# Gated linear attention: the two heads' products of a chunk regrouped by the number of rows they use

## The chip, the cores and the metric

The kernel runs on one core of one Trainium2 chip. The metric is device microseconds of one execution; the time before is the median of three runs. Beside them stands one profiled execution, from which every duration below is taken.

## The reference, cut to what matters

The kernel computes a whole decoder layer: a token mixer with three branches, a cross-attention and a mixture of experts. The change lies in the third branch of the mixer, gated linear attention, with 4 heads, 64 key columns and 128 value columns a head, 1024 tokens:

```
q_t = q * jnp.exp(cum)
k_t = k * jnp.exp(-cum)
attn = jnp.where(causal, jnp.einsum('bhnid,bhnjd->bhnij', q_t, k_t), 0.0)
intra = jnp.einsum('bhnij,bhnje->bhnie', attn, v)
k_dec = k * jnp.exp(cum[..., -1:, :] - cum)

def step(state, xs):
    qt_c, kd_c, v_c, cd_c = xs
    out = jnp.einsum('bhcd,bhde->bhce', qt_c, state)
    state = state * cd_c[..., None] + jnp.einsum('bhcd,bhce->bhde', kd_c, v_c)
    return state, out
```

The output of a chunk is its inner part (masked scores times values) plus what the state from the chunks before gives (queries times state).

## The kernel before, in words

gla_mix is called twice, once for each pair of heads. The keys and queries of a pair lie on 128 partitions, head 0 on rows 0 to 63 and head 1 on rows 64 to 127 (the list rows in the code), 1024 tokens along the free axis, in NT = 8 chunks of 128 tokens. All of its products are float32; each call is recorded as two weight loads and two matmuls.

The score part (L917 to L927) runs over head a, then over g, half of the chunks. Into one PSUM buffer of 128x4x128 it makes four products that use the 64 rows of the head (L923, 64 rows by 128 columns), then four that use 64 rows by 64 columns (L926); VectorE then copies the buffer under the mask into the scores AT of that head (L927). So the four groups a, g come one after the other, and each group holds two kinds of products.

Between, ScalarE and VectorE scale the queries and keys (L930 to L932), and TensorE transposes the keys (L938).

The chunk loop (L942 to L960) makes, for each chunk and head, po = qe times S (L947, 64 rows of the head, not for the first chunk) and adds AT times v to it (L948, all 128 rows); ScalarE copies po out (L949). Then for all but the last chunk the two heads' new key-value products go into one buffer, each on its own 64 columns (L954, 128 rows by 64 columns), and VectorE makes the next state S of it (L959, L957 for the first).

Around that, k.stream.fill(n) puts n steps of six matmuls each of the next projections into the program (L142 to L144, 128 rows by 128 columns, 512 moving columns): eight steps before the scores, two before the transposes, one in each chunk. A scheduler orders each engine's instructions when the kernel is built: the instruction that stands first in the program among those it takes to be ready. So the order on TensorE in the trace is not quite that of the program: L947 waits for S, and half of a step of projections stands ahead of it.

The pool k.ps has four PSUM buffers under the tag "s" that the scores, po and the state product share. Every buffer has the size of the largest tile of the tag, 128x4x128 float32.

After the second pair the kernel goes on with the projections up to the first head of the gated DeltaNet (gdn_mix), and so on to the end of the layer.

Of the kernel before, what the change touches and what calls it, by code (L numbers as in the profile page):

```python
# [8 lines left out]
F32 = mybir.dt.float32  # L9
# [35 lines left out]
def slot(k, name, shape=(128, T), dt=F32):  # L45

    return k.b4.tile(list(shape), dt, tag="b4", name=name)
# [611 lines left out]
def finish_out(k, on, sz, wc, oT, sq, spill=None):  # L659

    nc = k.nc
    ss = k.sm.tile([128, NT], F32, tag="rms_ss", bufs=2)
    for g in range(2):
        h = slice(g * 4, g * 4 + 4)
        nc.scalar.activation(sq[:, h], on[:, h], AF.Square)
        nc.vector.reduce_sum(ss[:, h], sq[:, h], axis=AX.X)
    r = k.sm.tile([128, NT], F32, tag="rms_r", bufs=2)
    rsqrt_cols(k, r, ss, NT, 128.0e-6)
    nc.vector.tensor_tensor(on, on, r[:, :, None].to_broadcast([128, NT, 128]), op=OP.mult)
    k.stream.fill(4)  # L670
    for g in range(2):
        ps = k.ptp.tile([128, 512], F32, tag="tp")
        for j in range(4):
            nc.tensor.transpose(ps[:, j * 128:(j + 1) * 128], on[:, g * 4 + j], k.ident)
        s = slice(g * HALF, (g + 1) * HALF)
        nc.vector.scalar_tensor_tensor(oT[:, s], ps, k.pcol[:, wc:wc + 1], sz[:, s], op0=OP.mult, op1=OP.mult)
    if spill is not None:
        nc.sync.dma_start(spill, oT)
# [210 lines left out]
def gla_mix(k, u, p, oT):  # L889
    nc = k.nc  # L890
    rows = (slice(0, 64), slice(64, 128))
    L = k.L

    def c3(t):
        return t.rearrange("p (c t) -> p c t", c=NT)

    def c4(t):
        return t.rearrange("p (c h t) -> p c h t", c=NT, h=2)

    c1, E, kt = c4(L.c1), c4(L.E), c3(L.kt)  # L900
    nc.vector.tensor_tensor_scan(L.c1, k.rm64, k.la[p], 0.0, OP.mult, OP.add)
    nc.scalar.activation(E, c1, AF.Exp, scale=1.0 / 16.0)
    nc.vector.scalar_tensor_tensor(u.q, L.E, 0.125, u.q, op0=OP.mult, op1=OP.mult)
    qt = c3(u.q)
    ee = k.sm.tile([128, NT, 2], F32, tag="l_ee", bufs=2)
    nc.vector.tensor_copy(ee, E[:, :, :, 63])
    cd = k.sm.tile([128, NT], F32, tag="l_cd", bufs=2)
    nc.vector.tensor_tensor(cd, ee[:, :, 0], ee[:, :, 1], op=OP.mult)
    nc.scalar.activation(E, c1, AF.Exp, scale=-1.0 / 16.0)
    nc.vector.tensor_tensor(L.kt, L.E, u.k, op=OP.mult)  # L910
    nc.vector.tensor_tensor(E, c1[:, :, :, 63:64].to_broadcast([128, NT, 2, 64]), c1, op=OP.subtract)
    nc.scalar.activation(E, E, AF.Exp, scale=1.0 / 16.0)
    nc.vector.tensor_tensor(u.k, L.E, u.k, op=OP.mult)
    kd = c3(u.k)
    k.stream.fill(8)

    for a in range(2):  # L917
        r = rows[a]
        for g in range(2):
            ps = k.ps.tile([128, 4, 128], F32, tag="s")  # L920
            for j in range(4):
                c = g * 4 + j
                nc.tensor.matmul(ps[:, j], kt[r, c], qt[r, c], start=True, stop=True)  # L923
            for j in range(4):
                c = g * 4 + j
                nc.tensor.matmul(ps[0:64, j, 64:128], kd[r, c, 0:64], qt[r, c, 64:128], start=True, stop=True)  # L926
            nc.vector.copy_predicated(L.AT[a][:, g * 4:g * 4 + 4], k.trii[:, None, :].to_broadcast([128, 4, 128]), ps)  # L927

    qe = c3(L.kt)
    nc.scalar.copy(qe[:, :, 0:64], qt[:, :, 0:64])  # L930
    nc.vector.tensor_tensor(qe[:, :, 64:128], qt[:, :, 64:128], ee[:, :, 0:1].to_broadcast([128, NT, 64]), op=OP.mult)
    nc.vector.tensor_tensor(kd[:, :, 0:64], kd[:, :, 0:64], ee[:, :, 1:2].to_broadcast([128, NT, 64]), op=OP.mult)  # L932
    kn = c3(L.E)
    k.stream.fill(2)
    for g in range(2):
        ps = k.ptp.tile([128, 4, 128], F32, tag="tp")
        for j in range(4):
            nc.tensor.transpose(ps[:, j], kd[:, g * 4 + j], k.ident)  # L938
        nc.scalar.copy(kn[:, g * 4:g * 4 + 4], ps)
    on = [c3(L.q2), c3(L.c1)]  # L940
    S = None
    for c in range(NT):  # L942
        for a in range(2):
            r = rows[a]
            po = k.ps.tile([128, 128], F32, tag="s")
            if S is not None:
                nc.tensor.matmul(po, qe[r, c], S[r], start=True, stop=False)  # L947
            nc.tensor.matmul(po, L.AT[a][:, c], u.v[a][:, c], start=(S is None), stop=True)  # L948
            nc.scalar.copy(on[a][:, c], po)  # L949
        k.stream.fill(1)  # L950
        if c < NT - 1:
            ps = k.ps.tile([128, 128], F32, tag="s")
            for a in range(2):
                nc.tensor.matmul(ps[rows[a]], kn[:, c, rows[a]], u.v[a][:, c], start=True, stop=True)  # L954
            Sn = L.small[:, 1 + c % 2]
            if S is None:
                nc.vector.tensor_copy(Sn, ps)  # L957
            else:
                nc.vector.scalar_tensor_tensor(Sn, S, cd[:, c:c + 1], ps, op0=OP.mult, op1=OP.add)  # L959
            S = Sn  # L960
    for a in range(2):
        finish_out(k, on[a], u.sz[a], 75, slot(k, "oc"), c3(L.kt), oT[2 * p + a])
# [1105 lines left out]
def hybrid_block(ctx, tc, ins, out):  # L2068
# [33 lines left out]
    with ExitStack() as c:  # L2102
        k.ps = c.enter_context(tc.tile_pool(name="psl", bufs=4, space=PSUM))
        for p in range(2):
            S.upto(f"l{p}")
            gla_mix(k, U[f"l{p}"], p, oT["c"])
# [114 lines left out]
```

## Time and profile before

| what | us |
|---|---|
| median of three runs | 2030.04 |
| lowest and highest of them | 2027.97, 2032.48 |
| the profiled execution | 2029.34 |
| its span, first to last instruction | 2027.6 |
| TensorE busy in the span | 1874.6 |

A row of the timeline gives the start, the time from the start of its first to the end of its last instruction, the engine, the line and operation, the tiles (out<-in), rows*columns of the array, the moving operand and the count; in brackets the idle time of the engine just before and what ended it. PE is the matmul, PEld the weight load of TensorE. Matmuls overlap in such rows: from the start of one to the start of the next is what one takes of the engine's time, and its own duration is longer.

### The profile page before, as it was taken

To read this page: it belongs to the slowest core of one execution; us is meant where nothing else is said; L and a number is where in the kernel's file an instruction comes from. 1 tells how busy PE (TensorE), PEld (TensorE's weight loads), DVE (VectorE), ACT (ScalarE), POOL (GpSimd) and SP (SyncE) were. 2 spreads that over 40 slices of the span, in tenths; PEclk is the share of its full clock that TensorE was granted. 3 is DMA by queue.
4 is the path that set the end of the run, shared out by engine and by line. 5 is a ranking of instruction groups with operands and counts; after the bars stand their busy time and mean duration, and the time that the engine had idled before them with its cause. 6 is when DMAs were issued, how large, how long until landed. Compare 5 with 4: busy or idle time off the path is not lost. (4 is left out here: it accounts for less than half of the span.)

```text
span 2027.6 us, 26514 instructions
## 1 busy us (share of the span) xinstructions
PE 1874.6 (92%) x9820; PEld 1521.3 (75%) x9820; DVE 1213.4 (60%) x2629; ACT 840.3 (41%) x1454; POOL 224.1 (11%) x261
## 2 busy tenths in 40 slices
PE   7999999999999999999989999899989689998890
PEld 6777787787877788888877788888877557876670
DVE  3244376676766543424455767544577648997885
ACT  3433232333332353535443312433421148876773
POOL 2000000000000010000003100000001222332310
PEclk8999999999999999999999999999999899999995
DMA  4113123232314122122525323710345577999995
GB/s 129 33 32 84 42 83 79 63 99 63 99 53 105 57 63 73 53 84 68 167 84 200 119 101 108 197 28 25 115 166 179 188 254 248 294 308 313 303 302 187
DMA packets 201653, 265.95 MB, mean 131 GB/s; under 512 B 24490, under 2 KB 132200, under 8 KB 201520
## 3 DMA queue, kind: packets, MB, share of 16 engines
q1 hardware_dynamic: 148992, 149.45, 23.6%
q10 hardware_dynamic: 39264, 86.07, 12.3%
q0 software_dynamic: 13264, 28.71, 6.0%
q8 instruction: 78, 1.28, 0.3%
q14 instruction: 55, 0.45, 0.1%
HBM read 228.95 MB, written 51.97 MB: 139 GB/s over the span
## 5 line engine op out<-in xcount | busy, mean ns | idle before, releaser
L142 PE MATMUL ps<-thh,hi 128*128 128x512 f32 x1152 | 467.7, 406 | 5.2 <-ACT hi L52 1.9
L143 PE MATMUL ps<-thl,hi 128*128 128x512 f32 x1152 | 456.4, 396 | 0.0
L144 PE MATMUL ps<-thh,lo 128*128 128x512 f32 x1152 | 455.7, 396 | 0.0
L142 PEld LDWEIGHTS ps<-thh,hi 128*128 128x128 f32 x1152 | 218.0, 189 | 51.5 <-issue 6.0
L144 PEld LDWEIGHTS ps<-thh,lo 128*128 128x128 f32 x1152 | 217.5, 189 | 45.8 <-issue 1.1
L143 PEld LDWEIGHTS ps<-thl,hi 128*128 128x128 f32 x1152 | 218.2, 189 | 38.8 <-issue 0.3
L1890 DVE TENSOR_TENSOR sl<-m_raw,sh 128x1024 fp32r<-128x1024 f32 x180 | 214.2, 1219 | 41.2 <-ACT sh L1887 31.6
L1887 ACT ACTIVATE sh<-m_raw 128x1024 fp32r<-128x1024 f32 x180 | 186.1, 1059 | 36.4 <-DMA acc<-m_y,r_big 13.0
L53 DVE TENSOR_TENSOR lo<-raw,hi 128x1024 fp32r<-128x1024 f32 x64 | 78.3, 1224 | 117.1 <-ACT hi L52 105.9
L52 ACT ACTIVATE hi<-raw 128x1024 fp32r<-128x1024 f32 x64 | 67.8, 1059 | 139.8 <-PE ps L143 120.1
L1646 PE MATMUL ps<-sl,m_xhi 128*128 128x512 f32 x240 | 97.6, 407 | 15.2 <-DVE sl L1890 14.5
L1645 PE MATMUL ps<-sh,m_xhi 128*128 128x512 f32 x240 | 101.1, 421 | 2.7 <-ACT sh L1887 2.7
L1647 PE MATMUL ps<-sh,m_xlo 128*128 128x512 f32 x240 | 95.9, 400 | 1.5 <-DVE m_xlo L1909 1.5
L783 DVE CUSTOM_DVE_ANT_0 f_P<-S,f_c 128x1024 f32<-128x1024 f32 (+7 forms) x64 | 48.4, 757 | 80.9 <-PE S L780 78.5
L1706 POOL DMA_INDIRECT acc<-m_y,r_big x32 | 60.3, 1883 | 205.8 <-ACT sh L1887 51.0
L1053 PE MATMUL ps<-ohi,hi 128*128 128x512 f32 x192 | 77.1, 402 | 1.5 <-DVE mt L1061 1.5
L791 ACT ACTIVATE f_P<-f_P,nm 128x1024 f32<-128x1024 f32 (+7 forms) x64 | 49.8, 778 | 65.7 <-DVE nm L783 65.4
L1055 PE MATMUL ps<-ohi,lo 128*128 128x512 f32 x192 | 75.5, 393 | 0.0
L1054 PE MATMUL ps<-olo,hi 128*128 128x512 f32 x192 | 75.3, 392 | 0.0
L1646 PEld LDWEIGHTS ps<-sl,m_xhi 128*128 128x128 f32 x240 | 45.9, 191 | 30.9 <-DVE sl L1890 22.4
L718 POOL TENSOR_SCALAR_AFFINE_SELECT f_c<-f_c 128x128 f32<-128x128 f32 x64 | 22.5, 351 | 388.8 <-DVE nm L783 363.6
L801 ACT COPY f_PT<-ps 128x512 f32<-128x512 f32 (+3 forms) x96 | 43.4, 479 | 46.1 <-PE ps L800 37.3
(489 smaller groups left out, 3733.2 us busy)
## 6 DMA issues: line engine op xcount, KB each, us to landing
raw<-in_w_in SPq DMA_DIRECT2D x64, 512.0 KB, 4.2
m_raw<-in_moe_w_down ACTq DMA_DIRECT2D x56, 512.0 KB, 5.9
m_raw<-in_moe_w_gate ACTq DMA_DIRECT2D x108, 256.0 KB, 5.9
m_raw<-in_moe_w_up ACTq DMA_DIRECT2D x108, 256.0 KB, 6.3
gate<-gt SPq DMA_DIRECT2D x24, 512.0 KB, 3.0
mt<-gate SPq DMA_DIRECT2D x24, 512.0 KB, 5.3
wraw<-in_xa_wkv SPq DMA_DIRECT2D x16, 512.0 KB, 7.5
m_raw<-in_moe_w_gate SPq DMA_DIRECT2D x20, 256.0 KB, 4.8
```

The source lines that it names most:

```text
L53: k.nc.vector.tensor_tensor(lo, src, hi.bitcast(F32), op=OP.subtract)
L142: k.nc.tensor.matmul(ps[:, :n], hi[:, d], xh, start=(d == 0), stop=False)
L143: k.nc.tensor.matmul(ps[:, :n], hi[:, d], xl, start=False, stop=False)
L144: k.nc.tensor.matmul(ps[:, :n], lo[:, d], xh, start=False, stop=(d == ND - 1))
L1053: nc.tensor.matmul(ps, whi[:, f], hi[:, s], start=(f == 0), stop=False)
L1054: nc.tensor.matmul(ps, whi[:, f], lo[:, s], start=False, stop=False)
L1055: nc.tensor.matmul(ps, wlo[:, f], hi[:, s], start=False, stop=(f == 3))
L1645: nc.tensor.matmul(ps, x[0], w[0], start=start, stop=False)
L1646: nc.tensor.matmul(ps, x[0], w[1], start=False, stop=False)
L1647: nc.tensor.matmul(ps, x[1], w[0], start=False, stop=stop)
L1887: nc.scalar.activation(w[e, i][0], raw[e][i], AF.Copy)
L1890: nc.vector.tensor_tensor(w[e, i][1], raw[e][i], w[e, i][0].bitcast(F32), op=OP.subtract)
```

## The change

The loops over heads move inward. In the scores g becomes the outer loop; both heads have a buffer, the eight products of L923 of a half come first, the heads alternating from product to product, then the eight of L926 in the same way, then both copies. In the chunk loop both po buffers are taken first; both heads' 128-row products (L948) come first and open the sum, then both heads' 64-row products (L947) close it, then both copies. No product, copy or load is added or removed.

```
-    for a in range(2):
-        r = rows[a]
-        for g in range(2):
-            ps = k.ps.tile([128, 4, 128], F32, tag="s")
-            for j in range(4):
-                c = g * 4 + j
-                nc.tensor.matmul(ps[:, j], kt[r, c], qt[r, c], start=True, stop=True)
-            for j in range(4):
-                c = g * 4 + j
-                nc.tensor.matmul(ps[0:64, j, 64:128], kd[r, c, 0:64], qt[r, c, 64:128], start=True, stop=True)
-            nc.vector.copy_predicated(L.AT[a][:, g * 4:g * 4 + 4], k.trii[:, None, :].to_broadcast([128, 4, 128]), ps)
+    for g in range(2):
+        ps = [k.ps.tile([128, 4, 128], F32, tag="s", name="ps") for a in range(2)]
+        for c in range(g * 4, g * 4 + 4):
+            for a, r in enumerate(rows):
+                nc.tensor.matmul(ps[a][:, c % 4], kt[r, c], qt[r, c], start=True, stop=True)
+        for c in range(g * 4, g * 4 + 4):
+            for a, r in enumerate(rows):
+                nc.tensor.matmul(ps[a][0:64, c % 4, 64:128], kd[r, c, 0:64], qt[r, c, 64:128], start=True, stop=True)
+        for a in range(2):
+            nc.vector.copy_predicated(L.AT[a][:, g * 4:g * 4 + 4], k.trii[:, None, :].to_broadcast([128, 4, 128]), ps[a])
...
     for c in range(NT):
+        po = [k.ps.tile([128, 128], F32, tag="s", name="po") for a in range(2)]
         for a in range(2):
-            r = rows[a]
-            po = k.ps.tile([128, 128], F32, tag="s")
-            if S is not None:
-                nc.tensor.matmul(po, qe[r, c], S[r], start=True, stop=False)
-            nc.tensor.matmul(po, L.AT[a][:, c], u.v[a][:, c], start=(S is None), stop=True)
-            nc.scalar.copy(on[a][:, c], po)
+            nc.tensor.matmul(po[a], L.AT[a][:, c], u.v[a][:, c], start=True, stop=S is None)
+        if S is not None:
+            for a, r in enumerate(rows):
+                nc.tensor.matmul(po[a], qe[r, c], S[r], start=False, stop=True)
+        for a in range(2):
+            nc.scalar.copy(on[a][:, c], po[a])
```

## Rows read from the trace of the kernel before

**Rows 1.** The page: the span, and part 1, busy time of each engine.

```profile
span 2027.6 us, 26514 instructions
PE 1874.6 (92%) x9820; PEld 1521.3 (75%) x9820; DVE 1213.4 (60%) x2629; ACT 840.3 (41%) x1454; POOL 224.1 (11%) x261
```

**Rows 2.** Busy time by stretch: length, then engines in order, PEclk, DMA.

```profile
120.00:265.00 145.00, 145.00 (x766) 110.37 (x766) 58.35 (x116) 42.48 (x84) 4.41 (x11) 1.00 0.20 51
```

**Rows 3.** Timeline of PE: the scores of the first pair, then of the second.

```profile
124.91 1.16 PE L923 MATMUL ps<-l_u,l_kt 64*128 64x128 f32 x8
126.00 0.68 PE L926 MATMUL ps<-l_u 64*64 64x64 f32 x8
...
131.67 0.50 PE L142 MATMUL ps<-thh,hi 128*128 128x512 f32 x1
...
218.16 1.16 PE L923 MATMUL ps<-l_u,l_kt 64*128 64x128 f32 x8
...
224.92 0.50 PE L142 MATMUL ps<-thh,hi 128*128 128x512 f32 x1
```

**Rows 4.** Timeline of PE at two instants: score products in flight.

```profile
125.12 0.50 PE L923 MATMUL ps<-l_u,l_kt 64*128 64x128 f32 x3
...
126.10 0.39 PE L926 MATMUL ps<-l_u 64*64 64x64 f32 x4
```

**Rows 5.** Timeline of PE over one chunk of the first pair.

```profile
138.60 0.49 PE L947 MATMUL po<-l_small,l_kt 64*128 64x128 f32 x2
139.01 0.49 PE L948 MATMUL po<-l_u,l_AT 128*128 128x128 f32 x2
139.43 0.48 PE L947 MATMUL po<-l_small,l_kt 64*128 64x128 f32 x2
139.85 0.49 PE L948 MATMUL po<-l_u,l_AT 128*128 128x128 f32 x2
...
140.63 0.40 PE L144 MATMUL ps<-thh,lo 128*128 128x512 f32 x1
140.96 0.44 PE L954 MATMUL ps<-l_u,l_E 128*64 128x128 f32 x4
141.33 0.50 PE L142 MATMUL ps<-thh,hi 128*128 128x512 f32 x1
141.66 0.39 PE L143 MATMUL ps<-thl,hi 128*128 128x512 f32 x1
...
142.22 0.48 PE L947 MATMUL po<-l_small,l_kt 64*128 64x128 f32 x2
```

**Rows 6.** Timeline of PE in a later stage: products on alternating 64-column halves.

```profile
714.97 0.55 PE L807 MATMUL ps<-f_PT,f_v 128*64 128x128 f32 x6
```

**Rows 7.** Lines L947 and L926: count, shortest, median and longest ns, first and last start.

```profile
L947 PE MATMUL po<-l_small,l_kt x56: 272/322/373, 138.6 to 255.3; 64*128 64x128 f32 x56
...
L926 PE MATMUL ps<-l_u x64: 218/218/267, 126.0 to 224.8; 64*64 64x64 f32 x64
```

**Rows 8.** Timeline of DVE and PE: the state, and the keys ahead of the transposes.

```profile
141.45 0.35 DVE L959 SCALAR_TENSOR_TENSOR l_small<-l_small,cd,ps 128x128 f32<-128x128 f32 x1 [3.33 <-PE ps L954]
...
131.78 0.73 DVE L927 COPY_PREDICATED l_AT<-l_small,ps 128x512 f32<-128x512 int32 x1
132.41 0.67 DVE L932 TENSOR_TENSOR l_u<-l_u,ee 128x512 f32<-128x512 f32 x1
...
134.32 0.39 PE L144 MATMUL ps<-thh,lo 128*128 128x512 f32 x1
134.55 0.27 PE L938 MATMUL ps<-ident,l_u 128*128 128x128 f32 x1
```

**Rows 9.** Timeline of ACT: copies of po out of PSUM.

```profile
139.54 0.27 ACT L949 COPY l_q<-po 128x128 f32<-128x128 f32 x1 [1.51 <-PE po L948]
```

**Rows 10.** Timeline after the branch: DVE, then PE, waits of the next stage.

```profile
310.42 0.69 DVE L517 TENSOR_REDUCE ss<-g_X 128x4 f32<-128x512 f32 x1 [4.98 <-ACT g_X L516]
...
348.84 0.36 PE L600 MATMUL ps<-g_Tn,g_LT 128*64 128x64 f32 x3 [1.87 <-DVE g_Tn L593]
```

## The prediction

> **What bounds the kernel now.** I read the page first: TensorE is busy for 1874.6 of 2027.6 us [rows 1]. That is an average over the whole layer, so the second view is the busy time of the stretch in which the changed branch runs: from 120 to 265 us matmuls cover all of the 145.00 us, the granted clock is 1.00 (the 2.4 GHz level), VectorE is busy for 58.35 and ScalarE for 42.48 us [rows 2]. So in this stretch only TensorE's own time counts. "Busy" doesn't say that it is busy at its best, though: matmuls overlap, and the third view, the timeline of TensorE, shows where one follows the other late. There the reader should compare distances from start to start.
>
> Products that use the same part of the array follow each other closely. Three of L923 span 0.50 us, and a matmul of this shape lasts 0.27, so they stand (0.50 - 0.27) / 2 = 0.11 us apart; four of L926 span 0.39, one lasts 0.22, so (0.39 - 0.22) / 3 = 0.06 apart [rows 4, 7]. Where the shape changes, the distance grows. In a chunk L947 starts at 138.60, L948 at 139.01, L947 at 139.43, L948 at 139.85 [rows 5]: 0.41 to 0.42 us for two matmuls that would take 0.22 at the close distance. Each visit to another shape thus costs 0.19 us: the second matmul comes 0.49 - 0.27 = 0.22 after the first, which is 0.10 late, and the next shape starts 0.20 after the second, which is 0.09 late. The same is seen where projections meet another shape: one of them and what follows it in the same shape start 0.23 apart (134.32 to 134.55) [rows 8], but 0.33 ahead of L954 (140.63 to 140.96) and 0.33 behind it (141.33 to 141.66) [rows 5]. Six shape changes lie in one chunk of 142.22 - 138.60 = 3.62 us.
>
> One more thing is in these rows: the four matmuls of L954, two heads on two 64-column halves, take 0.44 us, and the next line starts 0.37 after their first [rows 5]. Six of L807, also alternating between column halves, take 0.55 us; one by one at 0.11 they would take 5 x 0.11 + 0.27 = 0.82 [rows 6]. The two halves run at the same time: three pairs, two distances.
>
> **The change part by part.** Nothing is added or removed, so the whole effect is order.
>
> The chunk loop. New order in a chunk: L954 of the chunk before, both L948 (four matmuls, same shape as the projections), projections, both L947, projections. Four shape changes are left of six. Summing a chunk from the rows of before:
> - L954 with its way out: 140.96 to 141.33, 0.37.
> - Four matmuls of L948, the first of them after a change: 0.22 + 3 x 0.11 = 0.55.
> - Six projections at 0.23: 1.36.
> - Way out to the other shape: 0.10.
> - Both L947: if the two heads, on the upper and lower 64 rows of the array, run at the same time as the two column halves of L954 do, the block takes as long as one head does now, 0.41, and 0.01 for the shift: 0.42.
> - Way back in to projections and out to L954: 0.11 + 0.10.
>
> Sum 3.01 us against 3.62: 0.61 saved. How many projections stand ahead of L947 doesn't matter to this sum. L947 has 56 matmuls, four a chunk [rows 7], so 14 chunks have it (the first of each pair of heads has none): 14 x 0.61 = 8.5 us.
>
> The scores. Before, the scores of a pair take 131.67 - 124.91 = 6.76 us, and 224.92 - 218.16 = 6.76 for the second pair; that is four groups of 1.69, of which L923 takes 126.00 - 124.91 = 1.09 and L926 the other 0.60, changes included [rows 3]. After, two groups of each kind, with both heads in each. If the heads overlap, a group of 16 matmuls takes the time of one with eight and 0.01 more: 2 x (1.10 + 0.61) = 3.42. Saved 3.34 a pair, 6.7 us for both.
>
> What is not shown. The trace before has no place where two products on different 64-row halves stand next to each other; that they overlap is taken from the column halves [rows 5, 6], the nearest rows: same engine, same data type, half an array each. The bound on the other side is that they run one by one at the close distance. Then L947 takes 0.22 + 2 x 0.11 + 0.20 = 0.64, a chunk 3.23, saved 0.39, 5.4 us for 14; a score group 1.09 + 8 x 0.11 = 1.98 and 0.60 + 8 x 0.06 = 1.07, 6.10 a pair, saved 0.66, 1.3 us for both: 6.7 us in all. A third end lies below nothing and is a rival. I take the overlap, since the rows near it show no cost at all for going from one half to the other. The Trainium skill, "TensorE: Matmul & The Clock Gate", section "The mechanism", says of row groups that products in different ones overlap, with starts about 4 ns apart; by that the sum would be the same to 0.1 us, and no row of before shows it. Another page speaks against a free overlap: "TensorEngine Tiling (Array Packing)", "Gotcha 1: PSUM Pressure", says that different row tiles can't access one PSUM bank at the same time; by that, if the heads' outputs shared a bank, the sum would be the one-by-one 6.7.
>
> Waits. L948 no longer waits for S, and L947 has more ahead of it: from the start of L954 to the end of the state on VectorE is 141.45 + 0.35 - 140.96 = 0.84 us [rows 5, 8], and after the change L954 and both L948 alone take 0.37 + 0.55. So S is covered without any projections. If that cover were gone, each chunk would wait for what is missing, at most 0.5 us. Both po stay open until both L947 are done, so their copies come together; 0.27 us each [rows 9], on an engine that is busy for 42 of 145 us, ahead of 1 us or more of projections and L954. The four PSUM buffers hold two po, one state product and one more, so the second L948 of the next chunk waits for the first copy, which ends more than 0.5 us earlier. In the scores the last copy under the mask now has another, 0.73 us, ahead of it, and the scaling of the keys (L932) behind both must end before the transposes: now it ends at 132.41 + 0.67 = 133.08, 1.41 us behind the scores, and then 2.1, while the twelve projections between last 134.55 - 131.67 = 2.88 [rows 3, 8]. Still covered. Nothing is moved past a DMA queue: SP and POOL keep their order.
>
> What then follows is only shifted. The stretch after the branch starts from TensorE's projections: VectorE there sits idle for 4.98 us until ScalarE and TensorE deliver, and the first wait of TensorE is 1.87 us for VectorE, in the chain that starts there [rows 10]. So I carry the whole gain to the end.
>
> Sum: 8.5 + 6.7 = 15.2 us off the profiled execution's 2029.34 (its span 2027.6 and 1.7 around it): 2014.1. That execution is 0.7 under the median of the runs, so on the median 2030.04 - 15.2 = 2014.8 us.
>
> **The rivals.**
> - One by one: the row halves don't overlap, only shape changes are saved. 2030.0 - 6.7 = 2023.3. For it: no row shows the overlap. Against: L954 and L807 show it for columns [rows 5, 6].
> - Pulled apart: the scheduler puts projections between the two heads' L947, so the chunk keeps six changes, and only the scores gain: 2030.0 - 6.7 = 2023.3. Against: both become ready with the same S and stand side by side in the program.
> - Given back: the next stage's chain on VectorE takes no notice of an earlier TensorE, and the wait at 348.84 grows by the gain: 2030. Against: VectorE's own 4.98 us of waiting at 310 [rows 10].
> - A change of row half costs like a change of shape, 0.19 us, each time. It sits in the scores, where the heads now alternate: 7 changes in each of four groups, 28 a pair, and one in each of 7 chunks: 70 for both pairs, 13.3 us, against the 6.7 of the one-by-one case: 6.6 slower, 2036.6. It decides from 6.7 / 70 = 0.096 us a change. For it: all that I see of a change of shape, on rows too (L923 to L926). Against: none of the changes between column halves costs anything.
>
> **How the numbers follow.** The forecast 0.71, one by one 0.12, pulled apart 0.04, given back 0.05, slower 0.08. The forecast itself can shift by some 4 us, as the scheduler orders all that comes later anew. Range: down to 2009, and up to 2025.5, which takes in the two cases at 2023.3 and leaves out the other two, 0.13, and some of the forecast's tail. A measurement of this kernel can tell about 0.2%, 4 us. Faster by more than that is 0.71 + 0.12 + 0.04 = 0.87; within it 0.05; slower 0.08.
>
> **What would show it.** In the timeline of TensorE after: a score group of 16 matmuls in 1.16 us where eight stand now, the scores in 3.4 instead of 6.76 us; four matmuls of L947 together in 0.5 us with starts in pairs; chunks of 3.0 us; the first L600 some 15 us earlier with about the same wait. One by one would show as a score group of about 2.0 us, a costly change of halves as one of over 3. The prediction is wrong if L947 waits for S or for a buffer, or if the gain is there at 265 us and gone at the end.

## The result, and the profile after

The changed kernel takes 2010.93 us (median of 4 runs, 2009.19 to 2015.21); the kernel before, run beside it, 2030.28 (4 runs, 2027.97 to 2032.48). The ratio is 0.9908, interval 0.9887 to 0.9929, which on 2030.28 is 2007.3 to 2015.9 us. The forecast was 2014.8 with a range of 2009.0 to 2025.5: it held, near its low end, and the gain is some 4 us larger than forecast. The profiled execution took 2009.23 us, its span 2007.5, against 2029.34 and 2027.6.

The page of the changed kernel, part 1, busy time of each engine, to be read beside [rows 1]; and the windows of the branch (length; PE, PEld, DVE, ACT, POOL; granted clock; DMA share and GB/s), beside [rows 2]:

```profile
span 2007.5 us, 26509 instructions
PE 1854.4 (92%) x9820; PEld 1507.1 (75%) x9820; DVE 1212.0 (60%) x2629; ACT 838.3 (42%) x1454; POOL 222.0 (11%) x261
```

```profile
118.72:263.72 145.00, 145.00 (x837) 112.84 (x837) 69.28 (x126) 46.24 (x91) 4.39 (x11) 1.00 0.24 61
```

TensorE is still busy throughout at a granted clock of 1.00 (2.4 GHz), but 837 matmuls fit into 145 us where 766 did. Busy time can't show this, since it was full before and is full now; the count does.

The timeline of TensorE in the changed kernel, the scores of the first pair and one of its chunks, beside [rows 3] and [rows 5]. In the new numbering L921 and L924 are the score products, L944 is the 128-row product (before L948) and L947 the 64-row one:

```profile
123.63 1.16 PE L921 MATMUL ps<-l_u,l_kt 64*128 64x128 f32 x16
124.72 0.68 PE L924 MATMUL ps<-l_u 64*64 64x64 f32 x16
125.33 1.16 PE L921 MATMUL ps<-l_u,l_kt 64*128 64x128 f32 x16
126.42 0.68 PE L924 MATMUL ps<-l_u 64*64 64x64 f32 x16
127.03 0.50 PE L142 MATMUL ps<-thh,hi 128*128 128x512 f32 x1
...
132.70 0.44 PE L954 MATMUL ps<-l_u,l_E 128*64 128x128 f32 x4
133.07 0.71 PE L944 MATMUL po<-l_u,l_AT 128*128 128x128 f32 x4
133.54 0.48 PE L142 MATMUL ps<-thh,hi 128*128 128x512 f32 x1
133.95 0.49 PE L947 MATMUL po<-l_small,l_kt 64*128 64x128 f32 x4
134.37 0.50 PE L143 MATMUL ps<-thl,hi 128*128 128x512 f32 x1
...
135.73 0.44 PE L954 MATMUL ps<-l_u,l_E 128*64 128x128 f32 x4
```

Read it from start to start. Sixteen matmuls of L921 span 1.16 us, exactly what eight did before; sixteen of L924 span 0.68, also what eight did. The scores of the pair take 127.03 - 123.63 = 3.40 us instead of 6.76. In the chunk, four matmuls of L947 take 134.37 - 133.95 = 0.42, what two took, and the chunk lasts 135.73 - 132.70 = 3.03 (the next one, up to 138.75, 3.02) instead of 3.62. The overlap of the two row halves is there, at no visible price. It comes from the halves and not from the two PSUM buffers that the heads write: L944 writes the same two buffers with all 128 rows, and its four matmuls span 0.71 us against 0.49 for L947's four. One by one, four matmuls make three steps of 0.11; in two pairs they make one. The two spans differ by the two steps. What one buffer for both heads would do, no run shows.

Where the 20.1 us between the two profiled spans lie, from the starts of the same instructions in both timelines:

| stretch | before | after | difference |
|---|---|---|---|
| start of the span to the first score product | 124.91 | 123.63 | 1.28 |
| first score product to the projection behind the last po of the second pair | 130.87 | 115.21 | 15.66 |
| from there to the first L600 | 93.06 | 93.09 | -0.03 |
| first L600 to the first L616 | 7.81 | 4.84 | 2.97 |
| first L616 to the end | 1670.95 | 1670.70 | 0.25 |

The branch alone gives 15.66 us; two further pieces, 1.28 ahead of it and 2.97 behind it, were not forecast. The experiments are to say which part of the change gives how much, whether the overlap hangs on the alternation, and what the two further pieces are.

### The profile page after: what moved, and what is told of

Same layout as the page of the kernel before. It is cut to its first block, busy times and chain, and to the rows that moved or that the text cites. A ratio compares the mean times of both kernels' runs of the same rounds, so it can differ in the third digit from the quotient of the medians.

```text
span 2007.5 us, 26509 instructions
## 1 busy us (share of the span) xinstructions
PE 1854.4 (92%) x9820; PEld 1507.1 (75%) x9820; DVE 1212.0 (60%) x2629; ACT 838.3 (42%) x1454; POOL 222.0 (11%) x261
## 3 DMA queue, kind: packets, MB, share of 16 engines
q8 instruction: 78, 1.28, 0.3%
## 5 line engine op out<-in xcount | busy, mean ns | idle before, releaser
L1646 PE MATMUL ps<-sl,m_xhi 128*128 128x512 f32 x240 | 97.3, 405 | 17.1 <-DVE sl L1890 16.7
```

The source lines that it names most:

```text
L1646: nc.tensor.matmul(ps, x[0], w[1], start=False, stop=False)
```

## The experiments

One thing must be known ahead of the comparisons. Runs of one kernel spread by more than some of the effects: 40 runs of the kernel before, beside and among the experiments, lie between 2021.7 and 2038.9 us, and they follow the mean granted clock of the span (0.966 to 0.976): a straight line through them falls by 1.66 us per 0.001 of clock and leaves a scatter of 2.1 us. So beside the medians the table gives each kernel's mean distance from that line, "at equal clock"; by that scatter such a mean is uncertain by 0.7 us for 10 runs and by 1.1 for 4. A gain that comes through the clock itself is taken out by it. The lengths are from each kernel's own profiled execution; "branch" runs from the first score product to the instruction behind the last po.

| kernel | scores of a pair | chunk | branch | first scores to L600 | L600 to L616 | median us (runs) | at equal clock |
|---|---|---|---|---|---|---|---|
| before | 6.76 | 3.62 | 130.87 | 223.93 | 7.81 | 2030.28 (4) | 0 |
| the change | 3.41 | 3.02 | 115.21 | 208.30 | 4.84 | 2010.93 (4) | -16.5 |
| e1 scores only | 3.41 | 3.62 | 124.17 | 217.06 | 6.34 | 2021.36 (10) | -6.4 |
| e2 chunks only | 6.76 | 3.02 | 121.92 | 214.78 | 4.84 | 2018.84 (6) | -8.1 |
| e3 head blocks | 5.06 | 3.62 | 127.44 | 220.31 | 7.44 | 2027.16 (10) | -3.4 |
| e4 not grouped | 5.47 | 3.62 | 128.28 | 221.62 | 6.34 | 2029.17 (10) | -1.7 |
| e5 change again | 3.41 | 3.02 | 115.20 | 208.26 | 4.84 | 2011.01 (6) | -15.9 |
| e6 state next | 3.41 | 2.82 | 112.16 | 206.34 | 4.84 | 2007.32 (6) | -19.7 |
| e7 one shape all | 3.06 | 3.02 | 114.79 | 208.06 | 4.84 | 2010.16 (6) | -17.1 |
| e8 both | 3.06 | 2.82 | 111.66 | 205.70 | 4.84 | 2008.70 (6) | -19.9 |
| e9 before again | 6.76 | 3.62 | 130.87 | 224.34 | 6.35 | 2024.83 (1) | |
| e10 chunks again | 6.76 | 3.02 | 121.93 | 215.16 | 4.84 | 2015.65 (1) | -9.9 |

The kernel before took 2031.16 beside e1 to e4 (27 runs) and 2028.29 beside e5 to e8 (11 runs). The ratios below are those of the timed comparisons, with their 95% intervals; the medians take in every run, so their quotients differ a little. My theory: the gain is the overlap of the two heads' row halves and four shape changes a chunk instead of six, all on TensorE. The rivals: only the shape changes count; or it is the chunk order alone; or it lies in something behind the branch.

**The two parts alone.** e1 has the new scores and the old chunk loop, e2 the old scores and the new chunk loop. e1 keeps this part of the change:

```diff
-    for a in range(2):
-        r = rows[a]
-        for g in range(2):
-            ps = k.ps.tile([128, 4, 128], F32, tag="s")
...
+    for g in range(2):
+        ps = [k.ps.tile([128, 4, 128], F32, tag="s", name="ps") for a in range(2)]
+        for c in range(g * 4, g * 4 + 4):
+            for a, r in enumerate(rows):
+                nc.tensor.matmul(ps[a][:, c % 4], kt[r, c], qt[r, c], start=True, stop=True)
...
```

and e2 this one:

```diff
+        po = [k.ps.tile([128, 128], F32, tag="s", name="po") for a in range(2)]
         for a in range(2):
...
+            nc.tensor.matmul(po[a], L.AT[a][:, c], u.v[a][:, c], start=True, stop=S is None)
+        if S is not None:
+            for a, r in enumerate(rows):
+                nc.tensor.matmul(po[a], qe[r, c], S[r], start=False, stop=True)
...
```

> The new order of the score products alone; the chunk loop stays as before. If a visit to another shape costs 0.19 us and the two 64-row halves run at the same time, the scores of a pair take 3.4 instead of 6.76 us and the kernel gains 6.7 us, about 2023.5. If the gain of the whole change is a clock that happened to be better, the scores shorten all the same, but the time doesn't follow the scores: it stands anywhere from 2010 to 2030, with the mean granted clock of the execution.

> The new order of the chunk loop alone; the scores stay as before. Two changes of shape fewer and one overlap in each of 14 chunks: chunks of 3.02 instead of 3.62 us, 8.4 us gained, about 2021.9. With the scores-only kernel the gains should add up to the 15.1 us that the branch gained; what the whole change gained beyond that (some 4 us) should not appear in either, or should appear with the clock.

e1's ratio is 0.996 (0.9939 to 0.9981), e2's 0.993 (0.9903 to 0.9957). The timeline of TensorE in e1, scores and two starts of L953 (the state product there, a chunk apart), and then of e2, the last score group and two starts of L955, the same product:

```profile
125.06 1.16 PE L921 MATMUL ps<-l_u,l_kt 64*128 64x128 f32 x16
126.15 0.68 PE L924 MATMUL ps<-l_u 64*64 64x64 f32 x16
...
128.46 0.50 PE L142 MATMUL ps<-thh,hi 128*128 128x512 f32 x1
...
134.13 0.44 PE L953 MATMUL ps<-l_u,l_E 128*64 128x128 f32 x4
...
137.75 0.44 PE L953 MATMUL ps<-l_u,l_E 128*64 128x128 f32 x4
```

```profile
131.15 0.68 PE L926 MATMUL ps<-l_u 64*64 64x64 f32 x8
...
137.42 0.44 PE L955 MATMUL ps<-l_u,l_E 128*64 128x128 f32 x4
...
140.45 0.44 PE L955 MATMUL ps<-l_u,l_E 128*64 128x128 f32 x4
```

e1 has the scores at 3.40 and the chunk at 3.62, e2 the scores in groups of eight and the chunk at 3.03. In the branch they save 130.87 - 124.17 = 6.70 and 130.87 - 121.92 = 8.95, together 15.65, and the whole change saves 15.66: the parts add up, neither needs the other. (The 15.1 that the expectations name is the scores and 14 chunks alone; most of the rest of the 15.66 is two projections that move out of the branch, see below.) At equal clock they give 6.4 and 8.1, and the whole 15.9 to 16.5.

**Does the overlap hang on the alternation?** e3 groups the scores by shape as the change does, but inside a group takes head 0's four chunks and then head 1's four (in both product groups). e4 alternates the heads, but sends the 64-column products of a chunk right behind its 128-column ones, without grouping. Both have the old chunk loop, so they compare with e1. e3:

```diff
-        for c in range(g * 4, g * 4 + 4):
-            for a, r in enumerate(rows):
+        for a, r in enumerate(rows):
+            for c in range(g * 4, g * 4 + 4):
                 nc.tensor.matmul(ps[a][:, c % 4], kt[r, c], qt[r, c], start=True, stop=True)
```

e4:

```diff
                 nc.tensor.matmul(ps[a][:, c % 4], kt[r, c], qt[r, c], start=True, stop=True)
-        for c in range(g * 4, g * 4 + 4):
             for a, r in enumerate(rows):
                 nc.tensor.matmul(ps[a][0:64, c % 4, 64:128], kd[r, c, 0:64], qt[r, c, 64:128], start=True, stop=True)
```

> The scores grouped by shape as in the change, but head 0's four products stand ahead of head 1's four instead of alternating; the chunk loop stays as before. As many changes of shape as in the change. If products overlap only where they stand next to each other on different halves, a group runs nearly one by one: 2.0 us for the 128-column products and 1.1 for the 64-column ones, 6.1 a pair, 1.3 us gained, about 2028.9. If each half runs on by itself whatever the order, the scores take 3.4 us a pair as in the change, 6.7 us gained, about 2023.5.

> The heads alternate in the scores, but the shapes don't stay together: for each chunk both heads' 128-column product, then both heads' 64-column product, so 32 changes of shape in the scores of a pair instead of 8 before and 4 in the change; the chunk loop stays as before. If overlap and changes are two separate terms, a chunk takes 0.42 + 0.32 us, the scores of a pair 5.9 instead of 6.76: 1.7 us gained in all, about 2028.5. If the gain comes from fewer changes of shape alone and nothing overlaps, a chunk takes 0.64 + 0.43 and a pair 8.6: 3.7 us lost, about 2034.

The timeline of TensorE in e3, and below it in e4, first scores and what follows them:

```profile
125.00 1.71 PE L921 MATMUL ps<-l_u,l_kt 64*128 64x128 f32 x16
126.64 0.96 PE L924 MATMUL ps<-l_u 64*64 64x64 f32 x16
127.53 1.71 PE L921 MATMUL ps<-l_u,l_kt 64*128 64x128 f32 x16
...
130.06 0.50 PE L142 MATMUL ps<-thh,hi 128*128 128x512 f32 x1
```

```profile
125.09 0.49 PE L921 MATMUL ps<-l_u,l_kt 64*128 64x128 f32 x4
125.51 0.33 PE L923 MATMUL ps<-l_u 64*64 64x64 f32 x4
125.77 0.49 PE L921 MATMUL ps<-l_u,l_kt 64*128 64x128 f32 x4
...
130.55 0.50 PE L142 MATMUL ps<-thh,hi 128*128 128x512 f32 x1
```

In e3 a 128-column group takes 126.64 - 125.00 = 1.64 us. One by one it would be 1.98, fully overlapped it is 1.09 in the change. So (1.98 - 1.64) / 0.11, about three of the eight steps, overlapped. The 64-column group takes 0.89; one by one 0.60 + 8 x 0.06 = 1.08, so again (1.08 - 0.89) / 0.06, about three. Neither of the two expected times came (6.1 or 3.4 us a pair); 5.06 lies between. The timeline of TensorE just before and just after 125.555 us shows where the other half comes in:

```profile
125.33 0.50 PE L921 MATMUL ps<-l_u,l_kt 64*128 64x128 f32 x3
...
125.33 0.60 PE L921 MATMUL ps<-l_u,l_kt 64*128 64x128 f32 x4
```

Head 0's matmuls start at 125.00, 125.21 and then 0.11 apart, so the fifth starts at 125.55. Right beside it, at 125.555, one more joins those in flight. It ends at 125.33 + 0.60 = 125.93, so it lasts 0.37 us, the length of a half's first matmul (the longest in [rows 7]). So head 1 begins beside head 0's fifth matmul, with three of head 0's still ahead. The same 16 matmuls in the same shape group thus cost 0.55 us more for standing in blocks. The Trainium skill, "TensorE: Matmul & The Clock Gate", section "The mechanism", says that products in different row groups overlap, and that matmuls start in program order. In the program as built head 0's four products stand ahead of head 1's four; in that order head 1's first matmul could start only behind head 0's eighth, and the group would take the 1.98 of one by one. The measured 1.64 and the start at 125.55 decide: here the other half began three matmuls early, and the order in which they are issued still mattered.

In e4 a chunk takes 0.42 + 0.26 = 0.68 us, eight of them 5.46. It has 16 visits to a shape in a pair where the change has four: (5.46 - 3.40) / 12 = 0.17 us a visit, near the 0.19 read from the chunk in [rows 5]. (The 32 in the expectation is a miscount; its 5.9 is too long because the 64-column block took 0.26 and not 0.32.) So alternation without grouping gives 6.76 - 5.46 = 1.30 a pair, grouping without alternation 6.76 - 5.06 = 1.70, and both together 3.35. Two terms account for the three. Full overlap spares 16 steps of 0.11 and 16 of 0.06, 2.7 us a pair, and a visit costs 0.17. e4 has the full overlap, but 16 visits where the kernel before has 8: 2.7 - 8 x 0.17 = 1.3. e3 has 4 visits fewer and three eighths of the overlap: 0.7 + 1.0 = 1.7. The change has the full overlap and 4 visits fewer: 2.7 + 0.7 = 3.4. The ratios are 0.9967 (0.9948 to 0.9986) and 0.9979 (0.9959 to 0.9998), at equal clock 3.4 and 1.7 us against 3.43 and 2.59 in the branch; the timings alone could hardly tell these two apart, the timelines do. The Trainium skill, "TensorEngine Tiling (Array Packing)", section "Key Properties", says that a change of the tiling mode drains the engine while a change of tile does not. The rows agree: 0.17 to 0.19 us for a visit to another shape, none for going from one half to the other.

**The change again, and further along the same way.** e5 is the changed kernel once more. e6 goes one step further in the chunk loop: the state product stands right behind L947, ahead of the copies and of the projections, so that of the four shape changes of a chunk three are left. e7 does the scores of all eight chunks of a pair in one group a shape, on four PSUM buffers, and only then copies. e8 is both. e6:

```diff
-        for a in range(2):
-            nc.scalar.copy(on[a][:, c], po[a])
-        k.stream.fill(1)
         if c < NT - 1:
             ps = k.ps.tile([128, 128], F32, tag="s")
...
+        for a in range(2):
+            nc.scalar.copy(on[a][:, c], po[a])
+        k.stream.fill(1)
+        if c < NT - 1:
...
```

e7:

```diff
+    pss = [[k.ps.tile([128, 4, 128], F32, tag="s", name="ps") for a in range(2)] for g in range(2)]
+    for c in range(NT):
+        for a, r in enumerate(rows):
+            nc.tensor.matmul(pss[c // 4][a][:, c % 4], kt[r, c], qt[r, c], start=True, stop=True)
...
```

> The changed kernel itself, run more often beside the kernel before. In the branch it gained 15.1 us, the medians of the first runs stood 19.3 apart. Theory: the rest is the granted clock, which differs from execution to execution in both kernels; then at equal mean clock the two stand 15 to 16 us apart, and the mean clocks of many executions of both are about the same. Rival: the order itself gives a better clock or a shorter later stage; then the medians stand 19 us apart again, or the distance at equal clock is 19.

> The change, and in the chunk loop the state product of both heads stands right behind both heads' 64-row products, so the projections of a chunk are one block: three changes of shape in a chunk instead of four. If a change of shape costs the same wherever it lies, a chunk takes 0.11 + 1.37 + 0.45 + 0.10 + 0.42 + 0.37 = 2.82 instead of 3.02 us, 2.8 us less than the change. If the next chunk's products then wait for the state, which VectorE has to make in the meantime, nothing is gained or a chunk gets longer.

> The change, and the scores take all four buffers at once: all 16 products of 128 columns, then all 16 of 64 columns, then the four copies under the mask. Two changes of shape in place of four in the scores of a pair: 3.05 instead of 3.40 us, 0.7 us less than the change for both pairs, below what the runs can tell; the trace has to tell it. Rival: the four copies, 0.73 us each, now all come behind the products and the scaled keys behind them, so the transposes wait for VectorE and the gain is lost.

> The last two together: 3.5 us less than the change if they add up, at equal clock about 19 us under the kernel before.

e5 repeats the change: ratio 0.9907 (0.9881 to 0.9933), the branch 115.20, 15.9 us at equal clock and 17.3 between the medians, so the theory's 15 to 16 holds. The mean clocks are not quite the same, though: 0.9729 over the ten runs of the change, 0.9713 over the 40 of the kernel before, 2.6 us by the line. The timeline of TensorE in e6, one chunk:

```profile
134.72 0.49 PE L947 MATMUL po<-l_small,l_kt 64*128 64x128 f32 x4
135.14 0.44 PE L951 MATMUL ps<-l_u,l_E 128*64 128x128 f32 x4
135.51 0.50 PE L142 MATMUL ps<-thh,hi 128*128 128x512 f32 x1
...
137.00 0.60 PE L944 MATMUL po<-l_u,l_AT 128*128 128x128 f32 x4
137.54 0.49 PE L947 MATMUL po<-l_small,l_kt 64*128 64x128 f32 x4
```

The chunk takes 137.54 - 134.72 = 2.82, 0.20 less than in the change, one visit's price. The branch is 115.21 - 112.16 = 3.05 shorter, but L600 starts only 208.30 - 206.34 = 1.96 earlier: what lies between them takes longer by 1.1. Most of that is work that only moved: the branch of e6 holds 342 projections, that of the change 346, and 4 x 0.23 = 0.92. Nor could 14 chunks give 0.20 each, since the last chunk of a pair has no state product: 12 x 0.20 = 2.4, of which about 2.0 is seen at L600. The ratio is 0.9896 (0.9862 to 0.993); its 2007.32 stands beside 2011.0 for the ten runs of the change, 3.5 us less at equal clock, uncertain by 1.1. In e7 the scores of a pair take 3.06 instead of 3.41:

```profile
123.44 2.06 PE L920 MATMUL ps<-l_u,l_kt 64*128 64x128 f32 x32
125.43 1.15 PE L923 MATMUL ps<-l_u 64*64 64x64 f32 x32
126.50 0.50 PE L142 MATMUL ps<-thh,hi 128*128 128x512 f32 x1
```

These 0.35 us a pair are below what the runs can tell (0.9902, 0.9873 to 0.993; 2010.16). Nor do they all arrive: the branch is only 115.21 - 114.79 = 0.42 shorter, since the rival comes true in small part. VectorE, then TensorE, in e7:

```profile
128.64 0.68 DVE L931 TENSOR_TENSOR l_u<-l_u,ee 128x512 f32<-128x512 f32 x1
...
129.47 1.06 PE L937 MATMUL ps<-ident,l_u 128*128 128x128 f32 x8
```

The keys are ready at 129.32 and the transposes start at 129.47, 2.97 behind the scores (126.50) instead of 2.88. e8, with both, has the lowest ratio, 0.9885 (0.9857 to 0.9914), the shortest branch and the shortest way to L600, 208.30 - 205.70 = 2.60 less than the change where 3.5 was expected; it isn't told from e6 by its time. Either could be kept: by the intervals both overlap with the change, and what speaks for them is the shorter way to L600 besides the median.

**What is the rest of the gain?** The two pieces outside the branch stood in one execution each. e9 is the kernel before, e10 e2's kernel, each profiled once more, to see whether the clock behind L600 comes back the same.

> The kernel before once more, for a second profile. Of the ten profiles so far the four kernels with the old chunk loop (before, scores only, head blocks, not grouped) show TensorE at half clock behind its first wait for the next stage's chain (L600), and the time from L600 to L616 is 6.3 to 7.8 us; the six with the new chunk loop show the full clock there and 4.84 us. If that belongs to the order, it is there again: 6.3 or more. If it is an accident of an execution, it may be 4.84.

> The new chunk loop with the old scores once more, for a second profile. If the full clock behind L600 belongs to the order, 4.84 us from L600 to L616 again; if it is an accident of an execution, it may be 6.3 or more.

The timeline of TensorE around L600 in the changed kernel, then in e9 (in brackets what it waited before the group, in us, and for whom):

```profile
331.93 1.12 PE L600 MATMUL ps<-g_Tn,g_LT 128*64 128x64 f32 x16 [1.44 <-DVE g_Tn L593]
...
333.54 0.40 PE L142 MATMUL ps<-thh,hi 128*128 128x512 f32 x1
...
336.76 1.14 PE L616 MATMUL ps<-g_X,g_LT 64*64 64x64 f32 x16
```

```profile
348.49 1.11 PE L600 MATMUL ps<-g_Tn,g_LT 128*64 128x64 f32 x16 [2.26 <-DVE g_Tn L593]
...
350.47 0.63 PE L142 MATMUL ps<-thh,hi 128*128 128x512 f32 x1
...
354.85 1.14 PE L616 MATMUL ps<-g_X,g_LT 64*64 64x64 f32 x16
```

and the windows of that stretch, of the kernel before and of e10, with the granted clock as the third number from the end:

```profile
345.00:360.00 15.00, 13.13 (x88) 9.85 (x86) 6.34 (x11) 4.96 (x10) 0.00 (x0) 0.77 0.12 33
```

```profile
335.00:350.00 15.00, 13.44 (x103) 10.52 (x102) 9.37 (x15) 5.20 (x10) 0.00 (x0) 1.00 0.26 70
```

In e9 a projection behind L600 lasts 0.63 us, in the changed kernel 0.40: the first ran at the half clock (1.2 GHz), the second at the full one. All five profiles with the old chunk loop (before, e1, e3, e4, e9) show the drop, and 6.34 to 7.81 us from L600 to L616; all seven with the new chunk loop (the change, e2, e5 to e8, e10) show a granted clock of 1.00 and 4.84. So these 1.5 to 3.0 us come with the new order and are no luck of one execution. Why is not settled. The wait ahead of L600 is longer in all five that lost the clock (1.67 to 2.26 us idle; 1.87 in [rows 10]) than in all seven that kept it (1.19 to 1.66; 1.44 in the change), so its length goes with the clock in all twelve. But the two sets touch: it is 1.67 in e3, which lost the clock, and 1.66 in e6, which kept it, and no run changes this wait alone. That its length decides is argued and not shown.

The 1.28 us ahead of the scores is luck of the execution. The windows from 20 to 45 us, long before anything that the change touches, in the kernel before and then in the changed one:

```profile
20.00:45.00 25.00, 22.21 (x97) 17.30 (x96) 9.42 (x20) 8.69 (x19) 0.00 (x0) 0.91 0.20 53
```

```profile
20.00:45.00 25.00, 21.44 (x100) 16.50 (x99) 9.42 (x20) 8.69 (x19) 0.00 (x0) 0.99 0.20 53
```

The granted clock was 0.91 in one and 0.99 in the other. The first score product starts at 124.16 in e9, the kernel before, and at 124.61 in e6, which has the change; e2 and e10, one and the same kernel, stand at 124.99 and 123.62. This piece goes with neither order.

## Why the prediction was right, step by step

- **Overlap of the row halves**, the one step that no row of before showed: taken from the column halves of [rows 5] and [rows 6], and right. L947's four take 0.42 (forecast 0.42), a score group of sixteen 1.09 to its end (1.10), a pair 3.40 (3.42). One by one and a costly change of halves are both out, the first by 2.7 us a pair. What the step lacked is the condition that e3 showed: the two halves must alternate. The change does so, hence the forecast did not suffer.
- **The chunk**: 3.02 against 3.01, by the same items: L954 0.37, L947 0.42, and the 128-row product with six projections and the changes 2.24 against 2.22. The scheduler did not pull the two L947 apart.
- **Waits.** S comes in time. VectorE and then ScalarE in the chunk, from the changed kernel's timelines:

```profile
136.22 0.35 DVE L959 SCALAR_TENSOR_TENSOR l_small<-l_small,cd,ps 128x128 f32<-128x128 f32 x1 [2.74 <-PE ps L954]
...
137.49 0.27 ACT L949 COPY l_q<-po 128x128 f32<-128x128 f32 x1 [2.59 <-PE po L947]
137.66 0.27 ACT L949 COPY l_c<-po 128x128 f32<-128x128 f32 x1
```

  S is there at 136.57; L947 of that chunk starts at 136.97. From L954's start to S are 136.57 - 135.73 = 0.84, as forecast from before. L954 and both L944 alone take 0.84 as well (135.73 to 136.57), not the 0.92 that I reckoned: without the one projection between, the cover would have been just used up. The copies end at 137.93 and the next L944 starts only at 139.12, so the buffers hold nothing up. In the scores:

```profile
127.25 1.36 DVE L926 COPY_PREDICATED l_AT<-l_small,ps 128x512 f32<-128x512 int32 x2
128.50 0.68 DVE L931 TENSOR_TENSOR l_u<-l_u,ee 128x512 f32<-128x512 f32 x1
...
129.91 1.03 PE L937 MATMUL ps<-ident,l_u 128*128 128x128 f32 x8
```

  the keys are ready at 129.18, 2.15 us behind the scores (forecast 2.1), and the transposes begin at 129.91, 2.88 behind the scores as before.
- **The sum and where it goes.** The branch saves 15.66, forecast 15.2. The scores give 6.70 (6.7), the chunk loop 8.95 (8.5): 14 chunks at 0.60 are 8.40, and two projections (2 x 0.23) that the last chunks held are now behind the branch, where the wait ahead of L600 shrinks by 0.43 to make room for them. So that part is a true gain, and my sum had no term for it.
- **"Only shifted", with about the same wait at L600.** L600 starts 348.84 - 331.93 = 16.91 us earlier, 1.28 of it luck, and the gain isn't given back. But it isn't only shifted either: behind L600 another 1.5 to 3.0 us are gained, since the granted clock stays at 1.00. This is the step that was mis-sized. I carried the gain on as a plain shift, and didn't ask what granted clock the stretch behind a changed wait would have.

At equal clock the change gives 15.9 to 16.5 us, which is the branch; the rest of the 19.4 between the medians is granted clock. Part of that rest comes with the new order, behind L600, and part with the execution. How much is which in the timed runs isn't shown, since only the profiled ones show the clock by stretch.

## What to carry to other kernels

Where TensorE bounds a stretch and is "busy" throughout, read the distances from start to start by shape: here every visit to another shape cost 0.17 to 0.19 us, and products on different halves of the array ran side by side for nothing. So group by shape first, and alternate the halves inside the group: blocks of four chunks a half lost 0.55 us of what alternation gave in the same group, since only about three matmuls of a block overlapped. Small gains of this kind are read from timelines; one kernel's runs spread over 17 us with the mean granted clock.

## What the runs showed of the hardware that I had not expected

- The overlap of two row halves reaches only some three matmuls into a block of eight (e3: 1.64 us, and 0.89 in the 64-column group, by the same three), though the other half does begin before the block ahead of it in the program is through (head 1's first at 125.55, beside head 0's fifth).
- The granted clock behind one wait of TensorE was at half in five of five profiles with the old chunk loop (1.67 to 2.26 us idle) and at full in seven of seven with the new one (1.19 to 1.66). What decides it stays open.
- The time of one and the same program goes with its mean granted clock: 1.66 us per 0.001, over 40 runs.
